# Cross-entropy gradient over 8192 rows: every second block loaded by one 8 MB DMA, and the last stores issued from SyncE

## The chip, the cores and the metric

The kernel runs on one core of a Trainium2 chip. The metric is the device time of one execution in microseconds (us), the median of several runs; lower is better. The engines named below are VectorE (DVE), ScalarE (ACT), GpSimd (POOL), TensorE (PE) and SyncE (SP), which only waits and issues transfers here. Transfers between the chip's main memory (HBM) and the on-chip memory (SBUF) are made by 16 DMA engines. They are issued from a queue: those of SP are q1 in the profile, those of ACT are q10.

## The reference

Logits of 8 x 1024 rows with a vocabulary of 8192, labels of 8 x 1024. For each row: softmax minus the one-hot vector of the label.

```python
logits_max = np.max(logits, axis=-1, keepdims=True)
exp_logits = np.exp(logits - logits_max)
softmax = exp_logits / np.sum(exp_logits, axis=-1, keepdims=True)
one_hot[batch_idx, seq_idx, labels] = 1.0
return (softmax - one_hot).astype(np.float32)
```

Input and output are 268.4 MB each, in float32.

## The kernel before

The 8192 rows are cut into 32 blocks of 256 rows. In a block, partition p holds two neighbouring rows of the input, j = 0 and j = 1, so that the two lie next to each other in HBM, 64 KB together. The unit of work is "a row" t = 2 * block + j, from 0 to 63: one row of 8192 floats on each of 128 partitions, 4 MB. SBUF holds six of them in the tile X: three slots of two rows (`X[:, slot, j, :]`), and row t lives at place k = t % 6. Everything is done in place.

For each row:

- `load` (L114 to L118) issues one DMA on SP. From row 6 on it waits for the semaphore `put` of its place, which the store of row t - 6 raises by 16 when it has landed. It raises `got` of its place by 16. Row 5 waits instead for the iota table, which is made in that place first.
- `row_max` (DVE, L120) waits for `got` and takes the negated maximum.
- `row_exp` (ACT, L126) takes exp(x - max) in place, with the sum of the row beside it.
- `invert` (DVE, L132) takes the reciprocal of the sum.
- `row_scale` (ACT, L138) multiplies the row by it.
- `subtract` (DVE, L144) subtracts the one-hot vector: (iota == label) is made and subtracted in one pass.
- `store` (L151) issues one DMA on ACT's queue, after the subtraction.

The order on each engine is written by hand. SP issues the 64 loads one after the other (L158). DVE runs `invert(k)`, `row_max(k + 1)`, `subtract(k)` for each row (L173 to L180), so the next row's maximum stands before this row's subtraction. ACT runs `row_scale(k)`, `row_exp(k + 1)`, `store(k)` (L183 to L189). Ten rounds of six rows are loops; the last four rows (L191 to L210) are written out. The last row is scaled and subtracted in quarters, and stored in two halves, issued by ACT once all four quarters are scaled. Then ACT waits for all `put` semaphores (L211 to L213).

The helper `run` (L63) issues an instruction with its waits. As all instructions come from it, the profile shows most of them under L67, and they are told apart by their tiles: `m<-X` is `row_max`, `X<-X,m` is `row_exp`, `r<-s` is `invert`, `X<-X,r` is `row_scale`, `X<-iota,lab,X` is `subtract`.

Of the kernel before, what the change touches and what calls it, by code (L numbers as in the profile page):

```python
# [8 lines left out]
G = 2  # L9
SLOTS = 3  # L10
R = SLOTS * G


LAST = 4
# [3 lines left out]
def kernel(  # L18
# [6 lines left out]
    nc = tc.nc  # L25
# [8 lines left out]
    N, V = x_nv.shape  # L34
    T = N // P
    B = T // G
    lab_bp = labels.rearrange("a b -> (a b)").rearrange("(b q) -> b q", q=G * P)
    x_b = x_nv.rearrange("(b p j) v -> b p j v", p=P, j=G)
    o_b = o_nv.rearrange("(b p j) v -> b p j v", p=P, j=G)
# [5 lines left out]
    X = const.tile([P, SLOTS, G, V], fp32)  # L45
# [3 lines left out]
    lab = const.tile([P, G, B], fp32)  # L49
# [6 lines left out]
    with tc.tile_critical():  # L56
        sem = tc.alloc_semaphore
        got = [[sem(f"got{i}{q}") for q in range(2)] for i in range(SLOTS)]
        put = [[sem(f"put{i}{q}") for q in range(2)] for i in range(SLOTS)]
# [3 lines left out]
        def run(engine, waits, counter, method, **operands):  # L63

            for w in waits[:-1]:
                engine.wait_ge(*w)
            instruction = getattr(engine, method)(**operands)  # L67
            for w in waits[-1:]:
                instruction._wait_ge(*w)
            step = 16 if method == "dma_start" else 1  # L70
            instruction.then_inc(counter, step)
            count[counter.name] = count.get(counter.name, 0) + step
            return counter, count[counter.name]
# [6 lines left out]
            out=ident[:], in_=ident[:], compare_op=Alu.not_equal, fill=1.0,  # L80
# [10 lines left out]
        for j in range(G):  # L91
            w = run(
                nc.tensor, [w_ident, w_lab], pe, "transpose",
                out=lab_ps[:, j, :], in_=lab_f[:, j, :], identity=ident[:],
            )
        w_turned = run(nc.vector, [w], dve, "tensor_copy", out=lab[:], in_=lab_ps)
        w_iota = run(
            nc.vector, [w_turned, w_made], dve, "tensor_scalar",
            out=iota[:].bitcast(i32), in0=made.bitcast(i32), scalar1=0, scalar2=None, op0=Alu.bitwise_or,
        )  # L100


        def column(a, k):
            return a[:, k : k + 1]

        def per_row(name):
            return [sem(f"{name}{k}") for k in range(R)]

        max_of, exp_of, inv_of, scl_of, sub_of = map(per_row, ("max", "exp", "inv", "scl", "sub"))

        def slot(k):
            return X[:, k // G, k % G, :]

        def load(t):  # L114
            b, j = divmod(t, G)
            k = t % R
            free = [(put[k // G][k % G], t // R * 16)] if t >= R else [w_iota] if t == R - 1 else []
            run(nc.sync, free, got[k // G][k % G], "dma_start", out=slot(k), in_=x_b[b, :, j, :])  # L118

        def row_max(k, n):  # L120
            run(
                nc.vector, [(got[k // G][k % G], n)], max_of[k], "tensor_reduce",
                out=column(m, k), in_=slot(k), axis=mybir.AxisListType.X, op=Alu.max, negate=True,
            )

        def row_exp(k, n):  # L126
            run(
                nc.scalar, [(max_of[k], n)], exp_of[k], "activation", out=slot(k), in_=slot(k),
                func=Act.Exp, bias=column(m, k), scale=1.0, accum_out=column(s, k),
            )  # L130

        def invert(k, n):  # L132
            run(
                nc.vector, [(exp_of[k], n)], inv_of[k], "reciprocal",
                out=column(r, k), in_=column(s, k),
            )

        def row_scale(k, n, c=slice(0, V)):  # L138
            run(
                nc.scalar, [(inv_of[k], n)], scl_of[k], "activation", out=slot(k)[:, c],  # L140
                in_=slot(k)[:, c], func=Act.Copy, bias=0.0, scale=column(r, k),
            )

        def subtract(k, n, label, c=slice(0, V)):  # L144
            run(
                nc.vector, [(scl_of[k], n)], sub_of[k], "scalar_tensor_tensor",
                out=slot(k)[:, c], in0=iota[:, c], scalar=label, in1=slot(k)[:, c],
                op0=Alu.is_equal, op1=Alu.subtract, reverse1=True,
            )

        def store(k, n, target, c=slice(0, V)):  # L151
            run(
                nc.scalar, [(sub_of[k], n)], put[k // G][k % G], "dma_start",
                out=target[:, c], in_=slot(k)[:, c],
            )

        ROUNDS = T // R
        for t in range(T):  # L158
            load(t)
# [3 lines left out]
        def counter(engine, first, step):  # L163
            reg = engine.alloc_register(f"from{first}")
            engine.reg_mov(reg, first)
            return reg, step

        def advance(engine, counters):
            for reg, step in counters:
                engine.reg_add(reg, reg, step)  # L170

        n, got_n = counter(nc.vector, 1, 1), counter(nc.vector, 16, 16)
        with nc.vector.Fori(0, ROUNDS * SLOTS, SLOTS) as b:  # L173
            for k in range(R):
                invert(k, n[0])
                if k == R - 1:
                    advance(nc.vector, [got_n])
# [4 lines left out]
        n, next_n = counter(nc.scalar, 1, 1), counter(nc.scalar, 2, 1)  # L182
        with nc.scalar.Fori(0, ROUNDS * SLOTS, SLOTS) as b:  # L183
            for k in range(R):
                row_scale(k, n[0])
                row_exp((k + 1) % R, (n if k < R - 1 else next_n)[0])
                target = o_b[bass.ds(b + k // G, 1), :, k % G, :]
                store(k, n[0], target.rearrange("o p v -> (o p) v"))
            advance(nc.scalar, [n, next_n])  # L189

        n = ROUNDS + 1  # L191
        for t in range(ROUNDS * R, T):
            k = t % R
            label = lab[:, t % G, t // G : t // G + 1]
            target = o_b[t // G, :, t % G, :]
            invert(k, n)
            if t + 1 < T:
                row_max(k + 1, n * 16)
                row_scale(k, n)
                row_exp(k + 1, n)  # L200
                subtract(k, n, label)
                store(k, n, target)
            else:
                for q in range(4):
                    c = slice(q * V // 4, (q + 1) * V // 4)
                    row_scale(k, n, c)
                    subtract(k, n + q, label, c)
        half = V // 2
        store(k, n + 1, target, slice(0, half))
        store(k, n + 3, target, slice(half, V))  # L210
        for q in range(R):  # L211
            stores = [t for t in range(T) if t % R == q]
            nc.scalar.wait_ge(put[q // G][q % G], 16 * (len(stores) + (q == k)))  # L213


# [28 lines left out]
```

## Time and profile before

| | |
|---|---|
| median of 3 runs | 1248.07 us (1247.56 to 1248.09) |
| the profiled execution, its own time | 1247.74 us |
| the profiled execution, its span | 1245.8 us |
| DVE busy | 1120.4 us, 90% of the span |
| ACT busy | 919.4 us, 74% |
| bytes moved | 536.95 MB, mean 431 GB/s |
| `row_max`, mean of one | 8681 ns (64 of them) |
| `subtract`, mean of one | 8360 ns (67, the four quarters among them) |
| `row_exp`, mean of one | 7123 ns |
| `row_scale`, mean of one | 6816 ns (67, the four quarters among them) |

The profile is taken from one execution. Its span reaches from the first to the last recorded instruction; 1.9 us of the execution's own time lie outside it. In the views, times are us from the start of the span. A line of the timeline has the start, the duration, the engine ("ACTq" and "SPq" are the queues from which DMAs are issued), the source line, the operation, the tiles written and read, and in brackets the idle time of the engine before it and what ended that. The lines of DMA issues have the tiles, the queue, the number, the size of one and the median time from issue to landing. Each digit of the row "DMA" stands for a fortieth of the span: the busy share of the 16 engines in tenths, 9 for 90% or more.

The trace also has a record of each packet that a DMA engine moved, with its queue, size, start and end; where the text speaks of packet records, it means these.

### The profile page before, as it was taken

The numbers are of one execution on the slowest core, as the hardware profiler recorded it, in microseconds if no ns is written. First come the engines' busy times: TensorE is split into PE (matmuls) and PEld (weight loads), VectorE is DVE, ScalarE is ACT, GpSimd is POOL, SyncE is SP. The second block draws the span as 40 slices with busy tenths as digits, with TensorE's granted clock in tenths as the row PEclk, the third lists the DMA queues.
The fourth block names the chain that finished last, engine by engine and source line by source line (L and its number), as shares of the span: only waits on it lengthen the run. The fifth ranks groups of instructions, "written<-read, shape, count | busy, mean of one in ns | idle before, by whom it ended". The sixth has DMA issues, their size and how long they took to land.

```text
span 1245.8 us, 855 instructions
## 1 busy us (share of the span) xinstructions
PE 0.4 (0%) x2; PEld 0.3 (0%) x2; DVE 1120.4 (90%) x198; ACT 919.4 (74%) x196; POOL 7.4 (1%) x7
## 2 busy tenths in 40 slices
PE   0000000000000000000000000000000000000000
PEld 0000000000000000000000000000000000000000
DVE  5999999999988989889898898998988989889893
ACT  3888888888767777777767777777777777677772
POOL 2000000000000000000000000000000000000000
DMA  9999999999999999999999999999999999999999
GB/s 406 418 431 430 438 433 430 432 438 431 429 436 438 429 430 437 437 429 430 438 435 430 431 438 432 430 433 438 430 430 436 438 428 431 437 436 430 430 438 387
DMA packets 18625, 536.95 MB, mean 431 GB/s; under 512 B 2080, under 2 KB 2080, under 8 KB 2112
## 3 DMA queue, kind: packets, MB, share of 16 engines
q1 hardware_dynamic: 9216, 268.44, 50.0%
q10 hardware_dynamic: 9408, 268.51, 49.9%
q14 instruction: 1, 0.01, 0.0%
HBM read 268.50 MB, written 268.44 MB: 431 GB/s over the span
## 4 chain that ended last, share of the span: by engine, by line
another core or an unknown queue 67%; DVE 21%; DMA 6%; issue 2%; SPq 1%; DVEq 0%; ACT 0%; ACTq 0%; PE 0%
DVE m L67 11%; DVE X L67 10%; DMA out_dram<-X 4%; DMA X<-in_logits_dram 2%; SPq L67 1%; DMA lab_raw<-in_labels_dram 0%; DVE iota L67 0%; DVE lab_f L67 0%; DVEq L56 0%; ACT X L67 0%; DVE r L67 0%; PE iota L67 0%; ACTq L67 0%; DVEq L173 0%
## 5 line engine op out<-in xcount | busy, mean ns | idle before, releaser
L67 DVE TENSOR_REDUCE m<-X 128x1 f32<-128x8192 f32 x64 | 555.6, 8681 | 90.4 <-DMA X<-in_logits_dram 90.4
L67 ACT ACTIVATE X<-X,m 128x8192 f32<-128x8192 f32 x64 | 455.9, 7123 | 184.5 <-DVE m L67 184.5
L67 DVE SCALAR_TENSOR_TENSOR X<-iota,lab,X 128x8192 f32<-128x8192 int16 (+1 forms) x67 | 559.9, 8360 | 2.7 <-ACT X L67 2.7
L67 ACT ACTIVATE X<-X,r 128x8192 f32<-128x8192 f32 (+1 forms) x67 | 456.4, 6816 | 118.6 <-DVE r L67 118.6
L67 DVE RECIPROCAL r<-s 128x1 f32<-128x1 f32 x64 | 9.8, 153 | 7.3 <-ACT X L67 7.3
L67 ACT ACTIVATION_READ_ACCUMULATOR X<-X,m 128x1 f32 x64 | 12.0, 187 | 0.0
L67 DVE CAST lab_f<-lab_raw 32x256 f32<-32x256 int32 x1 | 2.4, 2366 | 6.0 <-DMA lab_raw<-in_labels_dram 6.0
L67 POOL IOTA X<- 128x8192 int16 x1 | 6.9, 6943 | 0.0
L67 DVE TENSOR_SCALAR iota<-X 128x4096 int32<-128x4096 int32 x1 | 4.4, 4428 | 0.1
L67 ACT ACT_TABLE_LOAD x1 | 1.3, 1283 | 1.4 <-SPq L56 1.4
L67 DVE COPY lab<-iota 128x64 f32<-128x64 f32 x1 | 0.2, 225 | 0.5 <-PE iota L67 0.5
L67 PE MATMUL iota<-ident,lab_f 32*128 32x32 f32 x2 | 0.4, 298 | 8.4 <-DVE lab_f L67 8.4
L67 PEld LDWEIGHTS iota<-ident,lab_f 32*128 32x128 f32 x2 | 0.3, 192 | 8.4 <-DVE lab_f L67 8.4
L67 POOL TENSOR_SCALAR_AFFINE_SELECT ident<-ident 32x32 f32<-32x32 f32 x1 | 0.2, 202 | 0.1
L67 POOL MEMSET ident<- 32x32 f32 x1 | 0.1, 114 | 0.5 <-SPq L56 0.5
L228 POOL MEMSET const-bfloat16-1.0<- 128x1 bf16 x1 | 0.1, 106 | 0.0
L228 POOL MEMSET const-uint8-127<- 128x1 uint8 x1 | 0.1, 106 | 0.0
L228 POOL MEMSET const-float32-0.0<- 128x1 f32 x1 | 0.1, 103 | 0.2 <-issue 0.2
L228 POOL MEMSET const-float32-1.0<- 128x1 f32 x1 | 0.1, 103 | 0.0
## 6 DMA issues: line engine op xcount, KB each, us to landing
X<-in_logits_dram SPq DMA_DIRECT2D x64, 4096.0 KB, 24.2
out_dram<-X ACTq DMA_DIRECT2D x63, 4096.0 KB, 55.1
out_dram<-X ACTq DMA_DIRECT2D x2, 2048.0 KB, 16.6
lab_raw<-in_labels_dram ACTq DMA_DIRECT2D x1, 64.0 KB, 5.1
```

The costliest lines, as they stand in the source:

```text
L67: instruction = getattr(engine, method)(**operands)
L228: nc = _bacc.Bacc("TRN2", target_bir_lowering=False, num_devices=1)
```

## The change

Blocks 4, 6, 8, ... 26 (`WIDE`) are loaded by one DMA of 8 MB, with one run of 64 KB on each partition, in place of two DMAs of 4 MB. Such a load waits for both `put` semaphores of its slot, that is for the stores of both rows which were there. The DMA raises `got` of row j = 0 when it has landed; `got` of row j = 1 is raised by an instruction of SP right behind the issue. DVE reaches the wait of row j = 1 only after that of row j = 0. The other 20 blocks are loaded as before.

In the end part the last row is scaled, subtracted and stored in two halves, each half stored as soon as it is subtracted. The stores of the last two rows, three DMAs, are issued by SP, and the last waits for all stores are SP's, too. DVE's and ACT's order in the loops is the same.

```diff
+WIDE = [4 <= b <= 27 and b % 2 == 0 for b in range(32)]
...
         def load(t):
             b, j = divmod(t, G)
             k = t % R
-            free = [(put[k // G][k % G], t // R * 16)] if t >= R else [w_iota] if t == R - 1 else []
-            run(nc.sync, free, got[k // G][k % G], "dma_start", out=slot(k), in_=x_b[b, :, j, :])
+            after = [(put[k // G][q], t // R * 16) for q in range(G)] if t >= R else []
+            if WIDE[b] and j == 0:
+                run(nc.sync, after, got[k // G][0], "dma_start", out=X[:, k // G], in_=x_b[b])
+                nc.sync.sem_inc(got[k // G][1], 16)
+            elif not WIDE[b]:
+                after = after[j : j + 1] or ([w_iota] if t == R - 1 else [])
+                run(nc.sync, after, got[k // G][j], "dma_start", out=slot(k), in_=x_b[b, :, j, :])
...
-        def store(k, n, target, c=slice(0, V)):
-            run(
-                nc.scalar, [(sub_of[k], n)], put[k // G][k % G], "dma_start",
+        def store(k, n, target, c=slice(0, V), queue=nc.scalar):
+            run(
+                queue, [(sub_of[k], n)], put[k // G][k % G], "dma_start",
                 out=target[:, c], in_=slot(k)[:, c],
             )
...
         n = ROUNDS + 1
-        for t in range(ROUNDS * R, T):
+        for t in range(ROUNDS * R, T - 1):
             k = t % R
-            label = lab[:, t % G, t // G : t // G + 1]
-            target = o_b[t // G, :, t % G, :]
             invert(k, n)
-            if t + 1 < T:
-                row_max(k + 1, n * 16)
-                row_scale(k, n)
-                row_exp(k + 1, n)
-                subtract(k, n, label)
-                store(k, n, target)
-            else:
-                for q in range(4):
-                    c = slice(q * V // 4, (q + 1) * V // 4)
-                    row_scale(k, n, c)
-                    subtract(k, n + q, label, c)
-        half = V // 2
-        store(k, n + 1, target, slice(0, half))
-        store(k, n + 3, target, slice(half, V))
+            row_max(k + 1, n * 16)
+            row_scale(k, n)
+            row_exp(k + 1, n)
+            subtract(k, n, lab[:, t % G, t // G : t // G + 1])
+            store(k, n, o_b[t // G, :, t % G, :], queue=nc.sync if t == T - 2 else nc.scalar)
+        k = (T - 1) % R
+        invert(k, n)
+        for q in range(2):
+            c = slice(q * V // 2, (q + 1) * V // 2)
+            row_scale(k, n, c)
+            subtract(k, n + q, lab[:, G - 1, B - 1 : B], c)
+            store(k, n + q, o_b[B - 1, :, G - 1, :], c, nc.sync)
         for q in range(R):
-            stores = [t for t in range(T) if t % R == q]
-            nc.scalar.wait_ge(put[q // G][q % G], 16 * (len(stores) + (q == k)))
+            rows = [t for t in range(T) if t % R == q]
+            nc.sync.wait_ge(put[q // G][q % G], 16 * (len(rows) + (q == k)))
```

## The prediction

> **What bounds the kernel now.** I read the page first: the slices, then the DMA queues.
>
> ```profile
> span 1245.8 us, 855 instructions
> DMA  9999999999999999999999999999999999999999
> GB/s 406 418 431 430 438 433 430 432 438 431 429 436 438 429 430 437 437 429 430 438 435 430 431 438 432 430 433 438 430 430 436 438 428 431 437 436 430 430 438 387
> ...
> q1 hardware_dynamic: 9216, 268.44, 50.0%
> q10 hardware_dynamic: 9408, 268.51, 49.9%
> ```
>
> All 16 DMA engines are busy in every slice. q1 carries the loads (SP), q10 the stores (ACT), half of the engines' time each. DVE is busy 90% of the span, ACT 74%. To see whether the rate depends on what is moved, I read stretches: loads alone, the steady state, stores alone. The columns after the stretch are its length, the engines' busy times, the clock, the DMA share and GB/s.
>
> ```profile
> 15.00:45.00 30.00, 0.00 (x0) 0.00 (x0) 22.72 (x4) 21.02 (x4) 0.00 (x0) 1.00 1.01 434
> 600.00:677.40 77.40, 0.00 (x0) 0.00 (x0) 69.61 (x13) 57.30 (x13) 0.00 (x0) 1.00 1.00 434
> 1235.00:1243.00 8.00, 0.00 (x0) 0.00 (x0) 0.00 (x0) 0.00 (x0) 0.00 (x0) 1.00 1.00 428
> ```
>
> About 434 GB/s in the first two; the third is short, and its landings below give the same rate. So the limit is that of the DMA engines, not of reading or writing. Then the waits (total us, times, longest), which show who waits for the DMA:
>
> ```profile
> DVE m L67 <- DMA X<-in_logits_dram: 90.4, 47, 2.0
> ```
> ```profile
> SPq L67 <- DMA out_dram<-X: 1140.2, 58, 57.2
> ```
>
> DVE waits some 2 us a row for a load; SP waits for a store before each load. Last, a steady stretch of the timeline:
>
> ```profile
> 578.32 8.69 DVE L67 TENSOR_REDUCE m<-X 128x1 f32<-128x8192 f32 x1 [1.95 <-DMA X<-in_logits_dram]
> 586.92 8.74 DVE L67 SCALAR_TENSOR_TENSOR X<-iota,lab,X 128x8192 f32<-128x8192 int16 x1
> ...
> 597.69 8.69 DVE L67 TENSOR_REDUCE m<-X 128x1 f32<-128x8192 f32 x1 [1.96 <-DMA X<-in_logits_dram]
> ```
>
> A row takes 597.69 - 578.32 = 19.37 us, of which DVE needs 17.3 (46.92 - 29.61 between two maxima in the stretch where it doesn't wait). In 19.37 us one row is loaded and one stored, 8.39 MB: 433 GB/s. Hence the time is: start of the first load, plus 128 row transfers of 9.68 us, plus the end. A change gains only if the transfers themselves become cheaper, and loses only if all queues are empty for a while.
>
> **Part 1: twelve blocks (4, 6, ... 26) loaded by one 8 MB DMA instead of two of 4 MB.** It removes 24 DMA issues on SP and adds 12, with 12 more waits and 12 semaphore increments there, each about as long as ACT's 29 ns register moves. SP is idle in waits for 1140 us, which hides them.
>
> *Price of the transfers.* The packet records of the trace have each partition's run as one packet: 8 per engine and row, 32768 B, and one 4 B completion write of 9 ns per engine and DMA. The last two store issues are halves, with packets of 16384 B. By the records, a row of 8 large packets passes in 9.681 us, a half of 8 packets half as long in 4.862. So 8 x 16384 B cost 9.681 - 4.862 = 4.819 us (435 GB/s over 16 engines), and 8 packets with their completion write cost 4.862 - 4.819 = 0.043 us whatever their size. A pair of rows now costs 2 x 9.681 = 19.362; 8 packets of 65536 B would cost 4 x 4.819 + 0.043 = 19.319. The gain is 0.043 us a block, 12 x 0.043 = 0.5 us. No row shows a 65536 B packet. Bounds: nothing gained (it is cut into two, 0), or all fixed cost of those rows gone (12 x 0.086 = 1.0). I take 0.5, the straight line through the two sizes measured.
>
> *What the later start costs.* A whole block waits for both stores of its slot pair, and DVE gets its first row only when 8 MB have landed. How these overlap now:
>
> ```profile
> X<-in_logits_dram SPq DMA_DIRECT2D x64, 4096.0 KB, 24.2
> out_dram<-X ACTq DMA_DIRECT2D x63, 4096.0 KB, 55.1
> ```
>
> The very first load lands 12.3 us after its issue, 9.7 of it transfer, so 2.6 us are fixed. Sharing the engines packet by packet a row takes 19.4, with the fixed part 22.0. Loads take 24.2, so each is queued about 2.2 us before its turn; stores take 55.1, so some 33 us of other stores lie ahead of each.
>
> The records show the engines taking one packet from q1, one from q10 in turn, each at 1.21 us. A packet of 65536 B then takes 2.42, and a whole block beside stores takes 8 x (2.42 + 1.21) = 29.0 us. In a period of four rows (one whole block, one of single rows) there are 32 store packets: 8 pass beside the whole block, 16 beside the two rows, and 8 are left to run alone, 9.7 us. 29.0 + 38.7 + 9.7 = 77.4 = 4 x 19.37: the load queue may stand empty for 9.7 us in each period at no cost, provided stores fill it. The 33 us of stores ahead, at half rate, are 16.5 us at full rate: enough for 9.7 plus the fixed 2.6.
>
> *The chain that must fit into 77.4 us* is from one whole block's landing to the next: the first row's maximum (8.6) and the subtraction of the row before (8.7), which stands behind it on DVE; the store of that row, the second of the slot pair that the next whole block needs (12.3 if it runs alone, 22.0 beside loads); that block's load (2.6 + 29.0). Sum: at most 17.3 + 22.0 + 31.6 = 70.9. That leaves 6.5 us, so no time is added. Behind the waiting maximum stand the subtraction, and behind that ACT's store issue; these come later in one lump: four times the 1.95 us that DVE idles now, 7.8 a period. In that lump it is the stores ahead that keep the engines busy. Cost 0; without that cover each period loses what the chain has over 77.4. The 10 single rows after block 26 even this out before the loads end.
>
> **Part 2: the end.** The last store issues now:
>
> ```profile
> 1215.55 0.34 ACTq L67 DMA_DIRECT2D out_dram<-X  x1
> 1216.26 7.68 ACT L67 ACTIVATE X<-X,r 128x2048 f32<-128x2048 f32 x4 [2.15 <-DVE r L67]
> 1218.30 9.13 DVE L67 SCALAR_TENSOR_TENSOR X<-iota,lab,X 128x2048 f32<-128x2048 int16 x4 [2.71 <-ACT X L67]
> 1222.94 4.86 ACTq L67 DMA_DIRECT2D out_dram<-X  x2
> ```
>
> They land 19.0 us after issue (1215.55), then 16.4 (1222.94) and 16.8 (1227.46), that is at 1234.6, 1239.3 and 1244.3: back to back, with 19.0 - 12.3 = 6.7, 16.4 - 2.6 - 4.9 = 8.9 and 9.3 us of queueing. The row in halves instead of quarters makes the first subtraction start one quarter of a scale later (1.9) and wait for a whole half (4.6): stores at 1224.7 and 1229.3 instead of 1222.9 and 1227.5, some 1.8 us later, hidden by 8.9 and 9.3. Moving three stores to SP saves ACT three issues of 0.34 us when nobody waits for ACT; SP issued its last load at 1173.9, so nothing stands behind them but each other and the last waits. Both queues drain through the same engines at the same rate. The waits' move from ACT to SP can alter only the 1.5 us between the last landing (1244.3) and the end of the span: between a gain and a loss of a few of ACT's semaphore steps, 0.3 either way. I take 0.
>
> **Sum.** 1245.8 - 0.5 + 0 + 0 = 1245.3 for the span; the profiled execution took 1247.74, so 1247.2; the median of the three runs is 1248.07, 0.33 above it: **1247.5**. The likeliest case has its own range of 1247.0 (1.0 gained) to 1248.1 (nothing).
>
> **Rivals.** *The queues run dry* (slower). Mechanism: a 65536 B packet does not get twice the share of a 32768 B one. A whole block then takes 2.6 + 38.7 = 41.3 beside stores, and the chain is 17.3 + 22.0 + 41.3 = 80.6, 3.2 over the 77.4. It decides once the chain passes 77.4. As the load queue then stands empty for part of the time, stores speed up by as much: the loss lies between 0 and half of 3.2, over 11 periods 0 to 18 us; the middle, 9, gives 1256.5. For it: no record has such a packet, and the margin of 6.5 us is thin beside 9.7. Against: the records alternate by whole runs of 32768 B. *It changes nothing*: the run is cut in two but the stores ahead absorb it; only 12 completion writes of 9 ns go, 1248.0. *Larger gain by rate*: to pass 2.5 us, a block must save 0.21 us of 19.36, 438 GB/s, above the 435 of the line through both packet sizes; say 1245. *Each DMA's fixed 2.6 us is paid in the queue*: 12 fewer, 31 us, 1217. Against it: DVE's rows follow every 19.37, the transfers alone being 2 x 9.64.
>
> The Trainium skill speaks for the last one: "DMA: Bandwidth & Descriptors", section "Anatomy of one DMA", fits a DMA issued from GpSimd as 2.0 us plus its bytes at 436 GB/s, and taken over to these queues would make this an estimated 12 x 2.0 = 24 us. By that fit the trace's rows would follow at 23 us; they don't, so the fixed part overlaps here. The same page, "Queues, rings and completion order", has each engine drain a whole packet from one row before it turns to the next, which is what the records show, and no run here shows it for 64 KB.
>
> **How the numbers follow.** Two runs here can be told apart from no change at about 0.2%, 2.5 us. Chances: forecast 0.69, nothing 0.09, dry queues 0.17 (0.03 of it below 2.5 us), larger rate 0.04, fixed cost 0.01. Faster 0.05, within 0.2% 0.81, slower 0.14. The range must leave out about 0.2: 1246.7 to 1250.6 holds the forecast, "nothing" and the small losses.
>
> **What would show it.** Right: q1 with 12 x 128 fewer large packets; rows in lumps, with DVE waiting about 8 us once in four rows; the load from issue to landing about 32 us for a whole block; DMA slices at 9 throughout; the last landings back to back. Wrong: a slice under 9 between 100 and 1200 us, q1 with as many packets as now, whole blocks taking 41 us, or rows more than 77.4 us apart per four.

## The result and the profile after

| | before | changed |
|---|---|---|
| median of 21 runs each | 1248.0 us (1247.55 to 1248.46) | 1250.12 us (1249.39 to 1250.62) |
| ratio, 95% interval | | 1.0018 (1.0012 to 1.0023) |
| span of the profiled execution | 1245.8 us | 1247.4 us |

The change costs 2.1 us (0.18%) where 0.5 were to be gained. The first views of the profile after look as forecast. The page:

```profile
span 1247.4 us, 863 instructions
DMA  9999999999999999999999999999999999999998
GB/s 406 419 429 438 429 437 437 425 450 420 436 440 421 435 434 436 442 418 435 435 434 433 430 437 435 428 433 434 452 419 431 433 433 434 434 430 435 433 434 365
...
q1 hardware_dynamic: 7920, 276.83, 51.5%
q10 hardware_dynamic: 8976, 260.12, 48.3%
q14 instruction: 2, 0.02, 0.0%
```

q1 had 9216 packets. The whole blocks take away 12 x 128 of them and 12 x 16 completion writes, and the three stores that moved to it bring the 9408 - 8976 = 432 that q10 has lost: 7920. So the whole blocks do move in 64 KB packets (the packet records have 1536 of 65536 B), and no slice but the last is under 9. The queue q14 carries fetches of instructions; it comes up again below. The issues, with the time to landing:

```profile
out_dram<-X ACTq DMA_DIRECT2D x62, 4096.0 KB, 34.7
X<-in_logits_dram SPq DMA_DIRECT2D x40, 4096.0 KB, 27.4
...
X<-in_logits_dram SPq DMA_DIRECT2D x12, 33.2
```

A whole block lands 33.2 us after its issue (31.6 were worked out), stores wait less. The lump of one period of four rows on DVE, from its timeline, and the waits:

```profile
455.12 0.15 DVE L69 RECIPROCAL r<-s 128x1 f32<-128x1 f32 x1
464.70 8.69 DVE L69 TENSOR_REDUCE m<-X 128x1 f32<-128x8192 f32 x1 [9.42 <-DMA X<-in_logits_dram]
473.30 8.74 DVE L69 SCALAR_TENSOR_TENSOR X<-iota,lab,X 128x8192 f32<-128x8192 int16 x1
```
```profile
DVE m L69 <- DMA X<-in_logits_dram: 96.4, 14, 9.4
```

DVE waits in lumps, 14 times up to 9.4 us instead of 47 times up to 2.0, and the sum is nearly the same (90.4 before). The stretches around such a lump show that the engines move on all the same: in the packet records the load queue is empty for 10.0 to 12.6 us before each whole block, here from 423 to 434.

```profile
422.50:433.50 11.00, 0.00 (x0) 0.00 (x0) 11.00 (x2) 9.85 (x2) 0.00 (x0) 1.00 1.02 441
433.50:443.50 10.00, 0.00 (x0) 0.00 (x0) 10.00 (x3) 8.17 (x3) 0.00 (x0) 1.00 1.02 439
443.50:463.00 19.50, 0.00 (x0) 0.00 (x0) 11.78 (x3) 16.27 (x4) 0.00 (x0) 1.00 0.99 429
463.00:501.50 38.50, 0.00 (x0) 0.00 (x0) 36.80 (x7) 23.28 (x6) 0.00 (x0) 1.00 1.01 435
```

So the mean over 16 engines hides the loss. It shows where the queues drain: 1240 to 1248 us in 40 slices of 0.2 us, before and after.

```profile
DMA  9799599599599573000000000000000000100000
GB/s 410 328 573 410 246 655 410 246 655 410 246 655 410 246 328 164 0 0 0 0 0 0 0 0 0 0 0 0 0 0 0 0 0 0 41 0 0 0 0 0
```
```profile
DMA  9979959939939511300100100000000000000000
GB/s 492 492 328 410 573 246 492 573 164 573 573 164 410 246 82 82 164 0 0 82 0 0 82 0 0 0 0 0 0 0 0 0 0 0 0 0 0 0 0 0
```

A figure of 82 is one packet of 16 KB in a slice (16384 B / 0.2 us). Before, all engines stop within a few slices. After, most stop as early, and one engine goes on alone, a packet each 0.6 us, for over a microsecond. The output is complete when that one is done.

The packet records give the engines' last landings, in us from the span's start: for each engine the end of its last completion write. (The prediction's 1244.3 was read from the store's semaphore, which comes some 0.5 us behind the last write, at 1243.77.) Whole blocks leave the middle engine where it was, and move the last one:

| run | first load packet | middle engine | last but one | last | span's end after that |
|---|---|---|---|---|---|
| before | 2.44 | 1243.30 | 1243.69 | 1243.77 | 2.04 |
| end part alone | 1.98 | 1243.08 | 1243.41 | 1243.68 | 2.67 |
| six whole blocks | 2.10 | 1243.15 | 1243.46 | 1244.60 | 2.55 |
| twelve whole blocks | 2.11 | 1243.02 | 1243.38 | 1246.15 | 2.06 |
| changed kernel | 1.97 | 1243.07 | 1243.82 | 1245.09 | 2.27 |
| changed kernel again | 1.96 | 1242.90 | 1244.37 | 1244.96 | 2.27 |
| changed kernel, last waits on ACT | 1.97 | 1243.00 | 1243.47 | 1245.82 | 2.05 |

The kernels of the other rows are described in the next section. These are single profiles; the last engine differs from run to run by a microsecond, and the profile with twelve whole blocks is the slowest of its 11 executions (1250.12 us, median 1249.40). From 100 to 1200 us the packet records before the change hold no idle gap on any engine, and those after the change hold a single one, of 0.30 us at a fetch of instructions: each engine always has a packet. An engine comes last mainly because its packets took longer.

### The profile page after: what moved, and what is told of

Same layout as the page of the kernel before. It is cut to its first block, busy times and chain, and to the rows that moved or that the text cites. A ratio compares the mean times of both kernels' runs of the same rounds, so it can differ in the third digit from the quotient of the medians.

```text
span 1247.4 us, 863 instructions
## 1 busy us (share of the span) xinstructions
PE 0.4 (0%) x2; PEld 0.3 (0%) x2; DVE 1115.4 (89%) x196; ACT 919.0 (74%) x194; POOL 7.4 (1%) x7
## 3 DMA queue, kind: packets, MB, share of 16 engines
q10 hardware_dynamic: 8976, 260.12, 48.3%
## 4 chain that ended last, share of the span: by engine, by line
DMA 64%; DVE 25%; issue 10%; ACT 0%; DVEq 0%; PE 0%; ACTq 0%; SPq 0%
DMA X<-in_logits_dram 34%; DMA out_dram<-X 29%; DVE X L69 16%; DVE m L69 8%; DMA lab_raw<-in_labels_dram 1%; DVE iota L69 0%; ACT X L69 0%; DVE r L69 0%; DVE lab_f L69 0%; DVEq L180 0%; PE iota L69 0%; DVE lab L69 0%; DVEq L177 0%; ACTq L190 0%; DVEq L69 0%
## 6 DMA issues: line engine op xcount, KB each, us to landing
X<-in_logits_dram SPq DMA_DIRECT2D x12, 33.2
```

## The experiments

**The end part alone.** `WIDE` is set to False for all blocks.

```diff
-WIDE = [4 <= b <= 27 and b % 2 == 0 for b in range(32)]
+WIDE = [False for b in range(32)]
```

> Only the end part of the change (last row in halves, last three stores and last waits on SP); all loads in 4 MB. Theory A (the whole blocks cost the 2.1 us: packets of 65536 B hold single DMA engines up): same as before, 1248.0 within 0.5 us, the last landing to the end of the span still about 1.5 us. Theory B (the end part costs it: stores and waits on SP): about 1250.1, ratio 1.0017, with the span's end further behind the last landing.

Measured: 1248.83 us against 1247.97, ratio 1.0007 (0.9998 to 1.0016). Neither theory's number: the median is 0.86 us up, with the ranges apart (1248.56 to 1249.04 against 1247.46 to 1248.37). Of it 0.55 lie in the median span (1246.6 against 1246.05) and 0.3 outside it (2.2 against 1.9), and the last landing is where it was.

**The whole blocks alone**: the kernel before with the changed `load`.

> Only the twelve whole blocks; the end part as before. Theory A: about 1250, ratio 1.0016, the last stores landing over 1 us later than before. Theory B: the 0.5 us of my forecast are gained, 1247.5, ratio 0.9996. Split between both: some 1249, ratio 1.0008.

Measured: 1249.40 us, ratio 1.0011 (1.0002 to 1.002): 1.43 us. With the end part's 0.86 that makes 2.29 for the changed kernel's 2.12, so the two parts add up, the whole blocks the larger. In this profile the engine that ends alone is easiest to see (1239 to 1249 us, slices of 0.25):

```profile
DMA  9999999799797961101001010010000000000000
GB/s 393 393 459 393 459 393 524 328 393 590 328 459 328 524 262 66 66 0 66 0 0 66 0 66 0 0 66 0 0 0 0 0 0 0 0 0 0 0 0 0
```

**Six whole blocks.**

```diff
-WIDE = [4 <= b <= 27 and b % 2 == 0 for b in range(32)]
+WIDE = [4 <= b <= 27 and b % 4 == 0 for b in range(32)]
```

> As the run with the whole blocks alone, but only six of them (4, 8, ... 24). Theory A with a price for each large packet: half of that run's difference. Theory A by chance of a few stalls: anything between. Theory B: 1247.8, no difference that can be measured.

Measured: 1249.07 us, ratio 1.0009 (1.0000 to 1.0018). 1.1 us for half the blocks is more than half of 1.43, but within what single microseconds can tell here. The records say it better. In the kernel before, one engine falls behind the first by 0.21 us at 360 us and by 0.84 at the end. With six whole blocks the last engine ends 1.75 us behind the first, with twelve 3.51. In the latter, 0.72 came at 1159 us, when an 8 KB fetch of instructions went through that engine (0.30 passed before its next packet, a load packet, and that took 0.41 longer). That leaves 0.9 us for six blocks and 1.95 for twelve over the 0.84: on average 0.15 to 0.16 us a block on this engine, against the 0.04 that every engine gains.

This average is not the price of a block's load alone. The lag of the last engine behind the middle one can be followed from store to store (by their landings, less whole packets where the order of the two queues on an engine shifts). With twelve blocks it grows from 0.27 us at 70 us to 2.40 at 1149. Some 1.1 of that appears in the stores right behind the twelve starts of a whole block, and the rest in between, 0.33 of it after 988 us, when no whole block is loaded any more; before the change the lag grows by 0.13 in the same time. With six blocks only 0.2 of 1.0 appears right behind the starts. Why an engine falls back faster in between, too, stays open.

The fetch is not peculiar to this run. The page before the change has one in the span, where that of the changed kernel (above) has two:

```profile
q14 instruction: 1, 0.01, 0.0%
```

In all profiles of kernels with the changed loads in twelve blocks a fetch falls between 954 and 1164 us, and a second one after 1200; in the others only the latter. In the changed kernel it stands at 1158 us, and the last engine's lag grows by 0.75 there. That is over half of the 1.32 us by which its last landing is later than before. Before the change the fetch, at 1220 us, goes through the engine that ends second last. Whether the longer program brings the additional fetch is not shown: no kernel here has the additional instructions without the later issue.

**The later issue with small packets.** In the same twelve blocks both rows stay loads of 4 MB, but each waits for both stores.

```diff
-            if WIDE[b] and j == 0:
-                run(nc.sync, after, got[k // G][0], "dma_start", out=X[:, k // G], in_=x_b[b])
-                nc.sync.sem_inc(got[k // G][1], 16)
-            elif not WIDE[b]:
+            if not WIDE[b]:
                 after = after[j : j + 1] or ([w_iota] if t == R - 1 else [])
+            if True:
                 run(nc.sync, after, got[k // G][j], "dma_start", out=slot(k), in_=x_b[b, :, j, :])
```

> No large packets: in the same twelve blocks each row is a 4 MB load as before, but its issue waits for both stores of the slot pair, as a whole block does. End part as before. If the large packets cost the time (theory A): 1248.0, ratio 1.0000. If the later issue costs it (rival C: lumps, skew between the engines): as the run with the whole blocks alone, 1249 to 1250.

Measured: 1252.46 us, ratio 1.0035 (1.0023 to 1.0047): worse than either theory said, in another place. 1222 to 1242 us in 40 slices:

```profile
DMA  9930100000009109090091917919199199938999
GB/s 393 524 131 0 66 0 0 0 0 0 0 0 983 66 0 1049 0 1049 0 0 999 66 983 66 328 655 66 983 66 590 393 66 492 524 524 164 360 524 524 524
```

From about 1223.5 to 1228 all engines stand nearly idle: the loads are late by the lumps of the steady part, and at the end no store is ready. The last landing is at 1248.56, and the engines are within 0.6 us of each other. Between 70 and 1140 us the packets of all engines together took 1.2 us longer than the usual 1.213 each, 2.418 for the large ones, from start to end (the next packet starts 0.004 before that end). The same sum is 0.6 us before the change, 1.8 with six whole blocks, 5.3 with twelve and 6.9 in the changed kernel; it is called the stretch from here on. So the stretch does not come with the later issue as such. The small spread at the end says nothing on that, as the engines start together again after they stood idle: at the store that lands at 1224 us the last engine is 1.74 us behind the first (before: 0.81), some 0.7 of it from an 8 KB fetch at 954 us. After the first blocks the load queue is never empty in this run: packets alternate one to one, and there is no restart, that is no start of the load queue after it stood empty beside stores that go on.

**The whole blocks cut at 32 KB.** One DMA of 8 MB and the same waits, but with X laid out as `[P, G, SLOTS, V]`.

```diff
-    X = const.tile([P, SLOTS, G, V], fp32)
+    X = const.tile([P, G, SLOTS, V], fp32)
...
-            return X[:, k // G, k % G, :]
+            return X[:, k % G, k // G, :]
...
-                run(nc.sync, after, got[k // G][0], "dma_start", out=X[:, k // G], in_=x_b[b])
+                run(nc.sync, after, got[k // G][0], "dma_start", out=X[:, :, k // G, :], in_=x_b[b])
```

> The twelve whole blocks with one DMA and the same waits, end part as before, but the tile X is laid out so that the two rows of a slot are not neighbours in SBUF: the run on a partition is cut at 32 KB. If large packets put one DMA engine back (theory A), its lag grows only as before, about 0.05 us in 77 us; but packets then alternate one to one, the loads come later, and the engines stand idle at the end for some us, as with the late pairs: 1250 to 1256. If the restart of an empty load queue is what puts it back, the lag grows by 0.1 to 0.2 us a block here, too. If it is still moved in 64 KB packets: as the run with the whole blocks alone, 1249.4.

Measured: 1258.36 us, ratio 1.0082 (1.0068 to 1.0095). All packets are of 32768 B, and a whole block takes 40.6 us from issue to landing (41.3 by the prediction's rival). The load queue is empty for 6.6 to 12.8 us before each block, and around a restart the rate falls:

```profile
202.00:214.00 12.00, 0.00 (x0) 0.00 (x0) 12.00 (x2) 9.66 (x3) 0.00 (x0) 1.00 0.99 390
214.00:226.00 12.00, 0.00 (x0) 0.00 (x0) 12.00 (x4) 10.22 (x2) 0.00 (x0) 1.00 0.97 396
```

Over the run the packets took 9.9 us an engine longer than usual (before: 1.2), which is 8.7 of the 10.35 us lost. Between 70 and 1140 us the stretch of all engines is 127.9 us: 42 lie within 3 us of a restart of the load queue, 45 within 3 us of one of the store queue, which runs empty for over 2.5 us 23 times here. Three engines end 1.2 to 1.7 us behind the middle one, not one alone, and the time is above the 1250 to 1256 expected. So packets are stretched at restarts without any large packet: the first form of theory A falls, and its rival, the restart, stands. That large packets add nothing of their own isn't shown, as no kernel here has them without restarts. In the run with twelve whole blocks 3.8 of the 5.3 us of stretch lie within the first 6 us of a block's load (with the packets that are under way when it starts), in the changed kernel 4.4 of 6.9; with six whole blocks only 0.5 of 1.8. Stretch where a queue starts beside another can be seen in the kernel before, too: as the first store sets in at 49 us, the load packets of each engine take some 0.6 to 1.2 us longer.

**The changed kernel once more.**

> The changed kernel once more for a second profile: about 1250.1. Theory A: once more 15 engines end their last store within some 1.5 us and one engine 1 to 3 us behind them. By chance: the last landings spread by 0.8 us, as in the profile of before.

Measured: 1249.43 us in one run. Its last landings spread by 2.5 us; one engine ends 0.6 us after the next, which is less than "1 to 3 us", and five more lie over 0.8 us behind the first. The lag isn't that of one engine alone in this kernel.

**The end part, taken apart.** Four kernels: only the last waits on SP; only the last three stores on SP; both; only the halves, on ACT.

Waits on SP, in the kernel before:

```diff
-            nc.scalar.wait_ge(put[q // G][q % G], 16 * (len(stores) + (q == k)))
+            nc.sync.wait_ge(put[q // G][q % G], 16 * (len(stores) + (q == k)))
```

> Of the end part only the last waits for the stores move from ACT to SP; all else as before. The run with the whole end part was 0.86 us slower, 0.55 in the span and 0.3 outside it. If the waits cost it: 1248.3 to 1248.8 with 2.2 us outside the span. If the stores on SP cost it: 1248.0 with 1.9 outside.

Stores on SP, in the kernel before, with the changed kernel's `store`:

```diff
-                store(k, n, target)
+                store(k, n, target, queue=nc.sync if t == T - 2 else nc.scalar)
...
-        store(k, n + 1, target, slice(0, half))
-        store(k, n + 3, target, slice(half, V))
+        store(k, n + 1, target, slice(0, half), nc.sync)
+        store(k, n + 3, target, slice(half, V), nc.sync)
```

> Of the end part only the last three stores move to SP's queue; quarters, order and the last waits (on ACT) as before. If the waits cost the 0.86 us: 1248.0. If the stores on SP do: 1248.3 to 1248.8, some of it outside the span.

Both of these edits together:

> Last three stores and last waits both on SP, the last row in quarters as before, no whole blocks. If it is the two moves together that end the program later (each alone did nothing): as the run with the whole end part, 1248.8, with 2.2 us outside the span. If the halves do it: 1248.0 with 1.9 outside.

The halves, in the changed kernel without whole blocks, with stores and waits back on ACT:

```diff
-            store(k, n, o_b[t // G, :, t % G, :], queue=nc.sync if t == T - 2 else nc.scalar)
+            store(k, n, o_b[t // G, :, t % G, :])
...
-            store(k, n + q, o_b[B - 1, :, G - 1, :], c, nc.sync)
+            store(k, n + q, o_b[B - 1, :, G - 1, :], c)
...
-            nc.sync.wait_ge(put[q // G][q % G], 16 * (len(rows) + (q == k)))
+            nc.scalar.wait_ge(put[q // G][q % G], 16 * (len(rows) + (q == k)))
```

> Only the halves: the last row is scaled, subtracted and stored in halves, with stores and waits on ACT (so the second half is scaled only after the first one's store is issued). No whole blocks. If the halves cost the 0.86 us: 1248.8. If the two moves to SP do: 1248.0, as the later issue is hidden by the 9 us in which these stores queue.

| run | median us | before beside it | ratio, 95% interval | outside the span |
|---|---|---|---|---|
| waits on SP | 1248.16 | 1248.01 | 1.0001 (0.9992 to 1.0010) | 1.9 |
| stores on SP | 1247.79 | 1248.01 | 0.9999 (0.9990 to 1.0008) | 1.9 |
| both on SP | 1248.54 | 1247.78 | 1.0006 (0.9997 to 1.0015) | 1.9 |
| halves, on ACT | 1248.22 | 1247.78 | 1.0004 (0.9995 to 1.0013) | 2.2 |

No ratio is outside its noise, but the medians have a pattern: either move alone changes 0.2 us or less, both together 0.8, nearly all in the span (1246.6 against 1245.9), and the profile has 2.67 us from the last landing to the span's end, as that of the whole end part. The halves add 0.3 outside the span and 0.1 in it. The queueing stores hid their later issue, as forecast: last landings at 1244.0 and 1243.8.

**The changed kernel with its last waits on ACT.**

```diff
-            nc.sync.wait_ge(put[q // G][q % G], 16 * (len(rows) + (q == k)))
+            nc.scalar.wait_ge(put[q // G][q % G], 16 * (len(rows) + (q == k)))
```

> The changed kernel with the last waits back on ACT; the stores stay on SP and the halves stay. If the end of the program is what the end part costs: 0.5 to 0.9 us less than the changed kernel's 1250.1, with 1.9 us outside the span, so about 1249.4, the price of the whole blocks alone. If not: 1250.1.

Measured: 1249.64 us, ratio 1.0013 (1.0004 to 1.0022). That is 0.5 us less than the changed kernel, but the kernel before, run beside it, was 0.2 lower, too (1247.78): over that it costs 1.86 us, against 2.12. The span's end is 2.05 us after the last landing instead of 2.27, and one engine lands 2.35 us behind the next; 2.2 us stay outside the span, so those belong to the halves, not to the waits. No version tried is faster than the kernel before by more than its noise.

## Why the prediction was wrong

*What bounds the kernel*: right as a rate, wrong as a sum. "Start of the first load, plus 128 row transfers of 9.68 us, plus the end" treats 16 engines as one. Each has its own sixteenth of the bytes and no slack, so a delay on one engine stays, and the end is set by the worst. This is the step that failed, together with the 0 that the later start was to cost. The sum was short before the change already: 2.44 + 128 x 9.681 + 2.04 = 1243.65, 2.2 us under the span, where stretched packets take 1.2 us an engine and the last engine lands 0.5 behind the middle one. What the runs showed in its place: the middle engine lands no later with whole blocks, and the last one does, by 1.32 us in the profile of the changed kernel and by 2.38 in that of the whole blocks alone. By the medians the whole blocks cost 1.43 us and the end part 0.86, whose interval still takes in no change. Not all of the mechanism is shown: restarts stretch packets, a fetch of instructions puts the last engine back by 0.7, and the rest of its lag grows between the whole blocks, for a reason that is open.

*Price of the transfers* (0.5 gained): right per packet. The records have one packet of 65536 B every 2.414 us where two of 32768 B took 2 x 1.209 = 2.418, so 8 x 0.004 = 0.03 and a completion write a block. As a gain of time it doesn't show: from the first load packet to the middle engine's last landing there are 1240.86 us before, 1241.10 with the end part alone, and 1240.91 to 1241.10 in the profiles with whole blocks. The stretch, 0.3 to 0.4 us an engine, is about as large as the gain.

*What the later start costs* (0): the cover held, and was sized well. Load queue empty 10.0 to 12.6 us before each block (9.7 and the fixed part), 3 to 4 store packets left on each engine when the block's load begins (the 16.5 - 12.3 us left are 3.5 packets), DVE lumps of 9.4 us (7.8), landing after 33.2 us (31.6). No engine ran empty. What I had not priced is that packets get stretched: 0.3 to 0.4 us an engine over the run on average (5.3 and 6.9 us over 16 engines, 0.6 before), most of it where a block's load starts beside the stores (3.8 and 4.4), and more on the engine that ends last. "Provided stores fill it" was not the only condition.

*The end part* (0, within 0.3): the landing was right, the end was not. The stores lost nothing, while the waits' and the stores' move together, and the halves, cost 0.86 us by the medians, after the last landing, in and outside the span. I had priced the waits' move alone, which does cost little (0.15). For the two moves together the profiles give a hint. In the three where the span ends latest after the last landing (2.55 to 2.67 us: the end part alone, both moves, six whole blocks) an 8 KB fetch of instructions falls between the two, at 1245.8, 1246.2 and 1246.9 us. In all the others (1.91 to 2.27 us) none does; before the change it comes at 1246.9, behind the end. The kernel with six whole blocks has the end part of before. So in these profiles the longer end goes with the fetch, and not with the moves as such; whether the fetch is the cause was not tried.

*The rivals*: "the queues run dry" did not happen here; no engine was without a packet. Its arithmetic was tested by the run cut at 32 KB: 40.6 us to landing and 1258.4 us, where it gave 41.3 and 1256.5. That the time came so near is in part luck: most of what that run lost are stretched packets, which the rival doesn't have. Its condition, that a large packet gets no double share, was wrong: the changed kernel's 33.2 us need the double share. The Trainium skill, "DMA: Bandwidth & Descriptors", section "Queues, rings and completion order", has an engine drain a whole packet before it turns to the next row; the trace agrees, up to 65536 B. "Each DMA's fixed part is paid in the queue" falls, too: 12 fewer DMAs brought nothing near 31 us.

*The range* held the time; the forecast's direction did not. Nearly all that was named as a sign of being right came (lumps of 9.4 us, whole blocks landing after 33.2, slices at 9), and the time still rose: none of these signs looks at the engines one by one.

Open: why one engine falls behind even before the change (0.6 us over 900), which one it is, whether it is the same in all runs (the records don't name it), and why it falls back faster in the kernels with whole blocks. The Trainium skill has, in "DMA: Bandwidth & Descriptors", section "Latency and other measured facts", that two of the 16 engines are usually slower, and suspects the GpSimd path; here no DMA goes that way and one engine lags all the same.

## What to carry to other kernels

Where a kernel is bound by DMA, look at the last landings engine by engine, not at the mean share: a busy share of 1.00 says nothing on how evenly the engines finish. Larger packets were worth little here: 64 KB instead of 32 KB saved 0.004 us a packet, 0.5 us in all, while the last engine landed 1.3 to 2.4 us later in the profiles of the changed kernel and of the whole blocks alone. A gain of half a microsecond is smaller than what one fetch of instructions on the wrong engine takes (0.7). When loads and stores share the engines, the size of a packet sets the share of its queue, and with that how long a load beside stores takes: 33.2 us for a whole block in large packets, 40.6 in small ones.

## What the runs showed of the hardware

- A queue with packets of 65536 B gets twice the time of one with 32768 B on each engine: whole blocks land after 33.2 us in large packets, 40.6 in small ones.
- 8 packets of 32768 B with their completion write take 9.681 us, of 16384 B 4.862: on an engine 4.819 us for 131072 B, and 0.043 for the rest whatever the size.
- One of 16 engines falls behind steadily, 0.6 us over 900, in a kernel that loads and stores evenly.
- A fetch of 8 KB of instructions takes a DMA engine out for 0.3 us, and in the run with twelve whole blocks it delayed that engine by 0.72, with a load packet behind it that took 0.41 longer.
- Where a queue starts beside another that is running, packets take longer: 0.6 to 1.2 us an engine as the first store joins the loads, and in the run cut at 32 KB 87 of 127.9 us of stretch lie within 3 us of such a start.
